# Two more pairs as block products in the last projection, with the weight sums made ahead and kept in HBM

## The chip, the cores and the metric

The kernel runs on one core of a Trainium2 chip. The metric is the device time of one execution in microseconds; the median of three runs before the change is 849.74 us (849.52 to 850.18).

## The reference

One trunk layer on x of 512 tokens by 1024 features, in float32:

```python
xn = rmsnorm(x, norm_mix_g)
q, k, v, xr, gr, ga, gb = split(xn @ w_in)
ya = chunked_band_attention(q, k, v, rel_table) @ w_attn_out
hr = rg_lru(causal_depthwise_conv(xr, conv_w, conv_b), ...)
yb = (hr * gelu(gr)) @ w_rnn_out
h = x + (sigmoid(ga + b_a) * ya + sigmoid(gb + b_b) * yb) @ w_o
hn = rmsnorm(h, norm_ffn_g)
g, up = split(hn @ w_ffn_in)              # 2 x 2816 columns
h = h + (silu(g) * up) @ w_ffn_out        # 2816 -> 1024: the last projection
return rmsnorm(h, final_norm_g)
```

The attention has 16 heads of 64; a frame sees its own chunk of 64 frames and the eight before it.

## The kernel before, in words

Every product of float32 matrices is made of three matmuls on rounded parts. An operand is split into a high part (a ScalarE copy) and a low part (what VectorE's subtraction leaves); mm3 at L76 to L78 multiplies high by high, high by low and low by high into one PSUM bank. A weight therefore goes through three steps: a load into a tile with the tag raw (three buffers, L167), the high part on ScalarE and the low part on VectorE (split, L82 and L83), into a tile with the tag whl.

The stages follow each other: the projections of the recurrent branch and its gates (the loop over j = 0, 2, 4, 6, two feature tiles at a time), q and k of the first head pairs, the recurrent branch's output (yb), v, the attention head by head with one q, k or gate tile between a head's transposes and its weighing, the attention's output, the merge with W_o, and the feed-forward part, whose input projection comes in six units.

Some products of two by two blocks are made with seven block products instead of eight (a scheme of Strassen and Winograd). It needs sums of the weight blocks: with blocks b11, b12, b21, b22 these are t1 = b12 - b11, t2 = b22 - t1, t3 = t2 - b11 and t4 = b21 - t2. For W_o and the first unit of W_ffn_in, sums_kept makes these sums early, inside the loop over j and behind k_tile(0), in four tiles b0 to b3 of the pool ob. It loads the four blocks (L285), subtracts on VectorE (L293 to L296), stores sums to HBM (L299), makes high and low parts of others (L303, L304) and stores them (L306); later stages load them from there. When the pool ob closes, the pool aw of the attention takes its memory; aw holds q and k of every second head pair, and the sums for v.

The last projection multiplies the 2816 activations, 22 tiles of 128 rows in eleven pairs, by W_ffn_out. Five pairs are plain: for each half of the 1024 columns, each of four token tiles and both rows of blocks there are three matmuls of 128x512. Six pairs (paired) are block products, where a block is 128 rows by 512 columns of the weight and 128 features by 256 tokens of the activation. Their weight pieces are fo0 (the first column half), t12 (t1 and t2), t3b (b22 - b12, and b22) and t4; out_sums loads rows of W_ffn_out and subtracts (L223, L225, L231, L237) before the parts are made. a_first, a_sums, a_second and a_last make the parts and sums of the activations. The order on TensorE: the first column half of the plain pairs, fo0 of the paired ones, the second half of two plain pairs, t12, one plain pair, t3b, t4, and two plain pairs last, so that the final norm can follow tile by tile.

What sets the order: in the attention and the feed-forward part TensorE's order, and in the last projection TensorE's and VectorE's, are those of the program text. Everywhere else a planner lists each engine's instructions by its own estimate of when they can start, the earlier in the text first. keep_in_program_order ties an instruction behind the one traced before it on its engine. SP issues nearly all transfers, in one list, and an engine stands still at an instruction whose inputs are late. prefetch makes the weight pieces in the order of the plan, as many pieces ahead as weights(name, ahead) says.

The instruction that follows the stores of the sums of W_ffn_in is the evacuation of k_tile(1): kh by ScalarE (L911), kl by VectorE (L912), in tiles of aw. The sums of x for v (x_sums, L945 and L947) are tied behind kl. whl_yb (L82, L83) are the weights of the recurrent output, v_t (L257, L258) sums of the weights of v, whl_v_t their parts.

In a head of the attention, bias_tile loads a bias of 256 KB (L703), GpSimd sets a corner of it (L704), scores adds it and takes the softmax, GpSimd scales the rows (L1057), and TensorE transposes them (L1068).

Of the kernel before, what the change touches and what calls it, by code (L numbers as in the profile page):

```python
# [8 lines left out]
F32 = mybir.dt.float32  # L9
# [5 lines left out]
P = 128  # L15
# [18 lines left out]
N_PLAIN = 5  # L34
PAIR_TILES = 2 * (11 - N_PLAIN)


@with_exitstack
def block_kernel(ctx: ExitStack, tc: tile.TileContext, x, norm_mix_g, w_in, b_merge, rel_table,
# [137 lines left out]
    t2_of, t2_room = {}, []  # L177
# [17 lines left out]

    def out_sums(name, rows):

        kind, i = name.split("_")
        if kind == "t4":
# [5 lines left out]
        def half_row(col):  # L205
            o = out_room[0].tile([P, S], F32, tag="half", bufs=3, name=f"half_{name}")
            sp.dma_start(out=o[:], in_=w_ffn_out[rows + P:rows + 2 * P, col:col + S])
            return o[:]

        if kind == "t12":  # L210
            raw = wp.tile([P, 2, S], F32, tag="raw", bufs=3, name=f"raw_{name}")
            sp.dma_start(out=raw[:], in_=w_ffn_out[rows:rows + P, :].rearrange("p (c n) -> p c n", c=2))
            b22 = half_row(S)

            if len(t2_of) < 2:
                if not t2_of:
                    t2_room.append(spare[0].tile([P, 2, S], F32, tag="act", bufs=13, name="t2_room"))
                t2 = t2_room[0][:, len(t2_of)]
            else:
                t2 = out_room[0].tile([P, S], F32, name=f"t2_{i}")[:]  # L220
            t2_of[i] = t2
# [4 lines left out]
            high_first(hl[:, 0, 1], hl[:, 1, 1], t1)  # L226
            high_first(hl[:, 0, 0], hl[:, 1, 0], t2)
        elif kind == "t3b":
            raw = wp.tile([P, 2, S], F32, tag="raw", bufs=3, name=f"raw_{name}")
            sp.dma_start(out=raw[:], in_=w_ffn_out[rows:rows + 2 * P, S:].rearrange("(k p) n -> p k n", p=P))  # L230
            dve.tensor_sub(raw[:, 0], raw[:, 1], raw[:, 0])  # L231
            low_parts()
            high_first(hl[:, 0], hl[:, 1], raw[:])
        else:
            b21 = half_row(0)
# [1404 lines left out]
```

## Time and profile before

| | before |
|---|---|
| median of three runs | 849.74 us |
| the profiled execution | 849.69 us |
| its span, first to last instruction | 847.9 us |
| TensorE busy | 839.1 us (99%) |
| VectorE busy | 663.2 us (78%) |
| ScalarE busy | 522.5 us (62%) |
| GpSimd busy | 140.6 us (17%) |
| moved by DMA | 137.17 MB, mean 162 GB/s |

The profile is that of one execution. A line of a timeline has the start in microseconds from the span's start, the duration in microseconds, the engine (PE is TensorE, DVE VectorE, ACT ScalarE, POOL GpSimd, SPq the transfers that SP issues), the line of the kernel, the operation, and what it writes and reads; in brackets stands how long the engine stood idle before it and what ended that. Ends of matmuls are modelled and overlap the next start, so that starts are what to read. The table by stretches gives the busy microseconds and the number of instructions of each engine in a stretch of time.

### The profile page before, as it was taken

The page shows a single profiled execution, that of the slowest core. Times are in us where ns is not written, and L with a number is a line of the kernel's source. Part 1 is how long each engine was busy: PE and PEld are TensorE (multiplying, and loading weights), DVE is VectorE, ACT ScalarE, POOL GpSimd, SP SyncE. Part 2 cuts the span into 40 slices and gives each one's busy share as a digit, 9 for nine tenths or more (in the row PEclk, how much of TensorE's full clock was granted, in tenths as well). Part 3 has the DMA queues.
Part 4 walks back from the last instruction along what each step waited for, and adds up shares of the span by engine and source line. Part 5 has one row for each costly group of instructions (what it writes and reads, how often), then busy time and mean ns, then how long its engine had stood idle before and what let it go on. Part 6 is the DMA issues. An engine that isn't in the chain of part 4 may idle for free.

```text
span 847.9 us, 11598 instructions
## 1 busy us (share of the span) xinstructions
PE 839.1 (99%) x4114; PEld 710.8 (84%) x4114; DVE 663.2 (78%) x972; ACT 522.5 (62%) x864; POOL 140.6 (17%) x179
## 2 busy tenths in 40 slices
PE   9999999999999999999999999999999999999996
PEld 6988888888888888888888888888888999888885
DVE  6667769886999788787568777888778878798995
ACT  7595848774466688787534568654664576645434
POOL 2412030221050133333000000003002213200000
PEclk9999999999999999999999999999999999999999
DMA  8433386777545433222233974555544445526642
GB/s 284 167 104 118 128 298 234 221 266 247 186 137 150 112 100 101 87 75 75 64 110 125 342 295 132 187 163 159 161 152 148 132 138 178 162 75 210 211 137 99
DMA packets 95385, 137.17 MB, mean 162 GB/s; under 512 B 7288, under 2 KB 62160, under 8 KB 94816
## 3 DMA queue, kind: packets, MB, share of 16 engines
q1 hardware_dynamic: 93696, 132.93, 48.9%
q10 hardware_dynamic: 1232, 2.95, 0.9%
q8 instruction: 32, 0.52, 0.3%
q0 software_dynamic: 400, 0.57, 0.3%
q14 instruction: 25, 0.20, 0.1%
HBM read 122.75 MB, written 13.67 MB: 161 GB/s over the span
## 4 chain that ended last, share of the span: by engine, by line
PE 82%; DVE 8%; ACT 4%; DMA 3%; issue 2%; ACTq 0%; DVEq 0%
PE fu_x L78 2%; PE fu_x L76 2%; PE fu_x L77 2%; PE po_out L76 2%; PE po_out L77 2%; PE po_out L78 2%; PE o L1088 2%; PE fg_x L78 2%; PE fg_x L76 2%; PE fg_x L77 2%; PE pT L1068 2%; PE po_ga L78 2%; PE po_ya L78 2%; PE po_ya L77 2%; PE po_ya L76 2%
## 5 line engine op out<-in xcount | busy, mean ns | idle before, releaser
L1288 POOL TENSOR_TENSOR sg<-sg,keep_fu_x 128x512 f32<-128x512 f32 (+1 forms) x10 | 17.8, 1782 | 238.8 <-DVE keep_fu_x L1287 238.8
L1057 POOL TENSOR_SCALAR p<-p,rl 128x128 f32<-128x128 f32 (+3 forms) x61 | 44.0, 739 | 14.9 <-DVE rl L1053 14.0
L1051 DVE CUSTOM_DVE_ANT_0 p<-s,bias 128x128 f32<-128x128 f32 (+1 forms) x64 | 28.6, 485 | 11.6 <-PE s L1043 10.2
L1052 ACT ACTIVATE p<-p,m 128x128 f32<-128x128 f32 (+1 forms) x64 | 35.5, 556 | 2.4 <-DVE m L1051 2.0
L76 PE MATMUL po_out<-whl_fo,act_hi 128*128 128x512 f32 (+1 forms) x80 | 30.9, 386 | 0.0
L78 PE MATMUL po_out<-whl_fo,act_lo 128*128 128x512 f32 (+1 forms) x80 | 30.7, 384 | 0.0
L77 PE MATMUL po_out<-whl_fo,act_hi 128*128 128x512 f32 (+1 forms) x80 | 30.7, 384 | 0.0
L83 DVE TENSOR_TENSOR whl_fu_w<-raw_fu_w,whl_fu_w 128x1024 fp32r<-128x1024 f32 (+1 forms) x18 | 22.1, 1227 | 8.5 <-ACT whl_fu_w L82 8.5
L83 DVE TENSOR_TENSOR pp<-pT,pp 128x384 fp32r<-128x384 f32 (+1 forms) x48 | 26.9, 596 | 2.0 <-ACT pp L82 1.8
L77 PE MATMUL po_xr<-xnT,whl_xr 128*128 128x512 f32 (+1 forms) x80 | 27.7, 353 | 0.0
L83 DVE TENSOR_TENSOR whl_fu_t<-t_fu,whl_fu_t 128x1024 fp32r<-128x1024 f32 (+1 forms) x18 | 23.8, 1324 | 4.8 <-ACT whl_fu_t L82 4.6
L77 PE MATMUL po_gr<-xnT,whl_gr 128*128 128x512 f32 (+1 forms) x80 | 27.5, 347 | 0.0
L78 PE MATMUL po_gr<-xnT,whl_gr 128*128 128x512 f32 (+1 forms) x80 | 27.3, 347 | 0.0
L78 PE MATMUL po_xr<-xnT,whl_xr 128*128 128x512 f32 (+1 forms) x80 | 27.2, 346 | 0.0
L76 PE MATMUL po_gr<-xnT,whl_gr 128*128 128x512 f32 (+1 forms) x80 | 27.1, 347 | 0.0
L76 PE MATMUL po_xr<-xnT,whl_xr 128*128 128x512 f32 (+1 forms) x80 | 26.3, 351 | 0.4 <-ACT xnT L615 0.4
L83 DVE TENSOR_TENSOR whl_fo<-raw_fo,whl_fo 128x1024 fp32r<-128x1024 f32 x16 | 20.7, 1304 | 7.7 <-ACT whl_fo L82 7.7
L82 ACT ACTIVATE whl_fu_w<-raw_fu_w 128x1024 fp32r<-128x1024 f32 (+1 forms) x18 | 17.8, 989 | 13.0 <-issue 7.1
L76 PE MATMUL po_k<-xnT,whl_qk 128*128 128x512 f32 x64 | 25.5, 398 | 0.0
L76 PE MATMUL po_q<-xnT,whl_qk 128*128 128x512 f32 x64 | 25.5, 398 | 0.0
L76 PE MATMUL po_ga<-xnT,whl_ga 128*128 128x512 f32 x64 | 25.4, 397 | 0.0
L82 ACT ACTIVATE whl_fu_t<-t_fu 128x1024 fp32r<-128x1024 f32 (+1 forms) x18 | 17.7, 988 | 12.6 <-PE fu_x L78 9.0
(614 smaller groups left out, 2994.9 us busy)
## 6 DMA issues: line engine op xcount, KB each, us to landing
raw_qk<-in_w_in_dram SPq DMA_DIRECT2D x32, 256.0 KB, 3.2
raw_fu_w<-in_w_ffn_in_dram SPq DMA_DIRECT2D x16, 512.0 KB, 4.4
raw_fo<-in_w_ffn_out_dram SPq DMA_DIRECT2D x16, 512.0 KB, 4.1
raw_xr<-in_w_in_dram SPq DMA_DIRECT2D x8, 512.0 KB, 5.7
raw_gr<-in_w_in_dram SPq DMA_DIRECT2D x8, 512.0 KB, 4.4
raw_ga<-in_w_in_dram SPq DMA_DIRECT2D x8, 512.0 KB, 3.8
raw_gb<-in_w_in_dram SPq DMA_DIRECT2D x8, 512.0 KB, 3.6
o_b<-in_w_o_dram SPq DMA_DIRECT2D x8, 512.0 KB, 6.9
```

What stands on the lines that cost most here:

```text
L76: pe.matmul(o, sh, mh, start=start, stop=False, skip_group_check=parts)
L77: pe.matmul(o, sh, ml, start=False, stop=False, skip_group_check=parts)
L78: pe.matmul(o, sl, mh, start=False, stop=stop, skip_group_check=parts)
L82: act.activation(hi, src, AF.Copy)
L83: dve.tensor_sub(lo, src, f(hi))
L1051: dve.tensor_tensor_reduce(prob[qb][:], scs[qb][:, 0:w], bias[:, S - w:S], -1.0, 3e38, ALU.add, ALU.min, nmax[:, qb:qb + 1])
L1052: act.activation(prob[qb][:], prob[qb][:], AF.Exp, bias=nmax[:, qb:qb + 1], scale=-1.0, accum_out=lsum[:, qb:qb + 1])
L1057: eng.tensor_scalar(prob[qb][:], prob[qb][:], rl[:, qb:qb + 1], 1.0, ALU.mult, ALU.mult)
L1068: pe.transpose(pt[:, at * P:(at + 1) * P], prob[qb][:, kb * P:(kb + 1) * P], ident[:])
L1088: pe.matmul(po[:, S - n:S], st, pp[i][:, part, lo:lo + n], start=kb == 0 and part == 0, stop=kb == NT - 1 and part == 1)
L1288: (pool if keep and (unit != f_units[-1] or side) else dve).tensor_mul(o, o, keep[a] if keep else banks[a])
```

## The change

Three pairs stay plain and eight become block products. The sums of their weights are made ahead by two new functions: out_blocks loads the two rows of blocks of the next pair (two loads of 512 KB), out_sums_kept makes four subtractions of 128x512 on VectorE and stores the result to HBM (two stores of 512 KB). They are called twice at the end of j = 0 and once at the end of j = 2, before sums_kept there, in the tiles b0 to b3 of ob; once between q_tile(0) and k_tile(0) in b2 and b3; and four times in the attention, in two of the three raw tiles: the loads after heads 0, 8, 10 and 12, the subtractions and stores after heads 1, 9, 11 and 13. In the last projection, out_sums loads the kept sums and makes only the high and low parts. The plan of the pieces has one plain pair less in the middle of the second column half. The order on TensorE holds back the second product of the last three pairs (two_sided) and takes t3b in two groups; the preparation of the activations is spread anew, and two activation tiles move into the room of the sums.

```diff
 CW = 256
-N_PLAIN = 5
-PAIR_TILES = 2 * (11 - N_PLAIN)
+N_PLAIN = 3
+PAIR_TILES = 2 * (11 - N_PLAIN) - (4 - (N_PLAIN - 1))
-    for i in plain[:-3]:
+    for i in plain[:-2]:
         plan_out(1, i)
     for i in paired:
         plan_block("t12", i)
-    plan_out(1, plain[-3])
+    out_kept = {i: dr.tile([2, P, D], F32, name=f"out_t{i}") for i in paired}
+    out_raw, t4_raw = {}, {}
+
+    to_keep = list(paired)
+
+    def out_blocks(pl=None, tags=("raw", "raw"), bufs=3):
+
+        i = to_keep.pop(0)
+        out_raw[i] = [(pl or wp).tile([P, 2, S], F32R, tag=tag, bufs=bufs, name=f"raw_out{i}_{n}")[:] for n, tag in enumerate(tags)]
+        out_raw[i] = [f(raw) for raw in out_raw[i]]
+        for n, raw in enumerate(out_raw[i]):
+            at = (2 * i + n) * P
+            sp.dma_start(out=raw, in_=w_ffn_out[at:at + P, :].rearrange("p (c n) -> p c n", c=2))
+
+    def out_sums_kept():
+
+        i = next(iter(out_raw))
+        one, two = out_raw.pop(i)
+        tc.keep_in_program_order(dve.tensor_sub(one[:, 1], one[:, 1], one[:, 0]))
+        dve.tensor_sub(two[:, 1], two[:, 1], one[:, 1])
+        dve.tensor_sub(one[:, 0], two[:, 1], one[:, 0])
+        dve.tensor_sub(two[:, 0], two[:, 0], two[:, 1])
+        for n, raw in enumerate((one, two)):
+            sp.dma_start(out=out_kept[i][n], in_=raw.rearrange("p c n -> p (c n)"))
+
...
+        if kind == "t4":
+            if i not in t4_raw:
+                raw = wp.tile([P, 2, S], F32, tag="raw", bufs=3, name=f"raw_{name}")
+                for n, i_ in enumerate(paired[i - paired[0]:][:2]):
+                    sp.dma_start(out=raw[:, n], in_=out_kept[i_][1, :, 0:S])
+                    t4_raw[i_] = raw[:, n]
+            raw = t4_raw[i]
+        else:
+            raw = wp.tile([P, 2, S], F32, tag="raw", bufs=3, name=f"raw_{name}")
         if kind == "t12":
-            raw = wp.tile([P, 2, S], F32, tag="raw", bufs=3, name=f"raw_{name}")
-            sp.dma_start(out=raw[:], in_=w_ffn_out[rows:rows + P, :].rearrange("p (c n) -> p c n", c=2))
...
-            t1 = raw[:, 1]
-            dve.tensor_sub(t1, raw[:, 1], raw[:, 0])
+            sp.dma_start(out=raw[:], in_=out_kept[i][:, :, S:].rearrange("c p n -> p c n"))
+        elif kind == "t3b":
+            sp.dma_start(out=raw[:, 0], in_=out_kept[i][0, :, 0:S])
+            sp.dma_start(out=raw[:, 1], in_=w_ffn_out[rows + P:rows + 2 * P, S:])
+        else:
             low_parts()
-            dve.tensor_sub(t2, b22, t1)
...
+            high_first(hl[:, 0], hl[:, 1], raw)
             return lambda part, k, at=every: hl[:, part, at]
+        low_parts()
+        high_first(hl[:, 0], hl[:, 1], raw[:])
         return lambda part, k, at=every: hl[:, part, k, at]
@@ loop over j, the recurrent branch @@
+        if j in (0, 2):
+            for tags in (("b0", "b1"), ("b2", "b3"))[j > 0:]:
+                out_blocks(obp, tags, 1)
+                out_sums_kept()
         if j:
             sums_kept(obp, "oof"[j // 2 - 1], (0, 1, 0)[j // 2 - 1])
@@ between the q and k tiles of the first head pair @@
     q_tile(0)
+    out_blocks(obp, ("b2", "b3"), 1)
+    out_sums_kept()
     k_tile(0)
     sums_kept(obp, "f", 1)
@@ attention @@
+    def kept_at(n, where):
+        if n in where and out_raw:
+            out_sums_kept()
+        if n + 1 in where and to_keep:
+            out_blocks()
...
                 probs[h + 2] = scores(h + 2)
             weigh(h, pp)
+            kept_at(h, (1, 9, 11, 13))
@@ last projection @@
+    spare_tags = ["t10", "t11", "t20", "t21"][N_PLAIN - 1:]
     ohp = []
 
     def pair_tile(i, name):
+        if spare_tags:
+            return sums_room.tile([P, 2, 2, 256], F32R, tag=spare_tags.pop(), bufs=1, name=f"{name}{i}")
         return ohp[0].tile([P, 2, 2, 256], F32R, tag="act", bufs=PAIR_TILES, name=f"{name}{i}")
-        todo = [what for i in paired for what in (lambda i=i: a_first(i), lambda i=i: a_sums(i))]
+        firsts = [lambda i=i: a_first(i) for i in paired]
+        sums = [lambda i=i: a_sums(i) for i in paired]
         for i in plain:
...
-                spread(todo, 3)
+                for _ in range(2):
+                    spread(firsts, 1)
+                    spread(sums, 1)
+                spread(firsts, 1)
         pq = [bank("s", f"p_out{a}") for a in range(2)]
-        for n, i in enumerate(paired):
-            w = weights(f"fo0_{i}", 4)
+        last_pairs = paired[-3:]
+
+        def two_sided(one, two, then=None):
+
+            held_ = []
+            for n, i in enumerate(paired):
+                one(n, i)
+                if i in last_pairs:
+                    held_.append(lambda n=n, i=i: two(n, i))
+                else:
+                    two(n, i)
+                if then:
+                    then(n)
+            for what in held_:
+                what()
+
+        pw = {}
+
+        def p_one(n, i):
+            pw[i] = weights(f"fo0_{i}", 4 if n < 4 else 2)
             if n == 0:
                 for t in (2, 3):
                     h_add(0, t, po[t][:])
             for a in range(2):
-                out_block(pq[a][:], left[i], 0, a, w, 0, n == 0)
+                out_block(pq[a][:], left[i], 0, a, pw[i], 0, n == 0)
+            if i == paired[-1]:
+                for a in range(2):
+                    h_add(0, a, pq[a][:])
+
+        def p_two(n, i):
             for a in range(2):
-                out_block(po[a][:], left[i], 1, a, w, 1, False)
+                out_block(po[a][:], left[i], 1, a, pw[i], 1, False)
+
+        def p_then(n):
+            spread(firsts, 1)
+            if n in (1, 3):
+                spread(sums, 1)
+
+        two_sided(p_one, p_two, p_then)
         for a in range(2):
-            h_add(0, a, pq[a][:])
             h_sum(0, a, po[a][:], 0)
         po = [bank("mm", f"po_out1_{t}") for t in range(NT)]
-        ws = [weights(f"fo1_{i}", 2) for i in plain[:-3]]
+        ws = [weights(f"fo1_{i}", 2) for i in plain[:-2]]
 
         for ts in ((2, 3), (0, 1)):
...
+            for i, w in zip(plain[:-2], ws):
                 for t in ts:
                     out_pair(po[t][:], t, i, w, i == 0)
...
         todo = [lambda i=i: a_second(i) for i in paired]
         qq = [bank("t", f"q_out{a}") for a in range(2)]
-        for n, i in enumerate(paired):
-            w = weights(f"t12_{i}", 4)
+
+        def t_one(n, i):
+            spread(sums, 1)
+            pw[i] = weights(f"t12_{i}", 4)
             for a in range(2):
-                out_block(pq[a][:], right_[i], 0, a, w, 0, False)
+                out_block(pq[a][:], right_[i], 0, a, pw[i], 1, False)
+            if i == paired[-1]:
+                for a in range(2):
+                    h_add(1, a, pq[a][:])
+
+        def t_two(n, i):
             for a in range(2):
-                out_block(qq[a][:], right_[i], 1, a, w, 1, n == 0)
-            spread(todo, 1)
+                out_block(qq[a][:], right_[i], 1, a, pw[i], 0, n == 0)
+
+        two_sided(t_one, t_two, lambda n: spread(todo, n > 0))
         for a in range(2):
-            h_add(1, a, pq[a][:])
             h_add(1, 2 + a, qq[a][:])
-        w = weights(f"fo1_{plain[-3]}", 5)
-        for t in range(NT):
-            out_pair(po[t][:], t, plain[-3], w)
-
-        h_add(1, 3, po[3][:, CW:S], slice(CW, S))
+        spread(todo, len(todo))
+        weights(f"t3b_{paired[-1]}", 0)
+        if plain[:-2]:
+            h_add(1, 3, po[3][:, CW:S], slice(CW, S))
         for i in paired:
             a_last(i)
-        weights(f"t4_{paired[-1]}", 0)
+        weights(f"t4_{paired[3]}", 0)
         g_fin = acp.tile([P, D], F32, tag="act", bufs=13, name="g_fin")
         pool.dma_start(out=g_fin[:], in_=final_norm_g.partition_broadcast(P))
...
         ws = [weights(f"t3b_{i}", 0) for i in paired]
-        for w, i in zip(ws, paired):
-            for a in range(2):
-                out_block(pq[a][:], left[i], 0, a, w, 0, False)
-        for a in range(2):
-            h_add(1, 2 + a, pq[a][:])
-        for w, i in zip(ws, paired):
-            for a in range(2):
-                out_block(qq[a][:], left[i], 1, a, w, 1, False)
+        pairs_ = list(zip(ws, paired))
+        for some in (pairs_[:-6], pairs_[-6:]):
+            for w, i in some:
+                for a in range(2):
+                    out_block(pq[a][:], left[i], 0, a, w, 0, False)
+            if some is not pairs_ and len(some) == 6:
+                for a in range(2):
+                    h_add(1, 2 + a, pq[a][:])
+                weights(f"t4_{paired[-1]}", 0)
+            for w, i in some:
+                for a in range(2):
+                    out_block(qq[a][:], left[i], 1, a, w, 1, False)
```

More of the change, by code (lines that the diff above doesn't have):

```diff
@@ L203, in out_sums @@
             hl = out_home(name)
[L205 to L208, printed above, removed]
-        if kind == "t12":
-            raw = wp.tile([P, 2, S], F32, tag="raw", bufs=3, name=f"raw_{name}")
-            sp.dma_start(out=raw[:], in_=w_ffn_out[rows:rows + P, :].rearrange("p (c n) -> p c n", c=2))
[L213 to L221, printed above, removed]
-            t1 = raw[:, 1]
-            dve.tensor_sub(t1, raw[:, 1], raw[:, 0])
-            low_parts()
-            dve.tensor_sub(t2, b22, t1)
[L226 to L235, printed above, removed]
-            t2 = t2_of[i]
-            dve.tensor_sub(t2, b21, t2)
-            low_parts()
-            high_first(hl[:, 0], hl[:, 1], t2)
```

6 lines of the change are left out of this document (3 added, 3 removed).

## The prediction

> **What bounds the kernel now.** I read the first lines of the page, then TensorE's timeline in the last projection, then the busy time by stretches, then who waited for whom around 200 to 250 us, and last the price of each kind of transfer and subtraction.
>
> ```profile
> span 847.9 us, 11598 instructions
> ...
> PE 839.1 (99%) x4114; PEld 710.8 (84%) x4114; DVE 663.2 (78%) x972; ACT 522.5 (62%) x864; POOL 140.6 (17%) x179
> ```
>
> The execution with this span took 849.69 us, so 1.79 us lie around it; the median of the runs is 849.74, 0.05 above. A busy TensorE alone says little, since the modelled ends overlap. The starts of its matmuls say more:
>
> ```profile
> 744.72 0.39 PE L77 MATMUL po_out<-whl_fo,act_hi 128*128 128x512 f32 x1
> ...
> 756.74 0.39 PE L76 MATMUL p_out<-whl_fo,left 128*128 128x512 f32 x1
> ...
> 789.15 0.39 PE L78 MATMUL q_out<-whl_t,right 128*128 128x512 f32 x1
> ```
>
> These are 197 matmuls in a row, all 128x512: 44.43 us over 196 steps, 0.2267 us a step, with no gap. The plain pairs end and the block products begin at 756.74. TensorE sets the time here, and nearly everywhere:
>
> ```profile
> 40.00:60.00 20.00, 20.00 (x94) 16.03 (x93) 12.15 (x15) 17.54 (x25) 2.92 (x3) 1.00 0.43 134
> ...
> 120.00:140.00 20.00, 20.00 (x94) 16.03 (x93) 14.46 (x17) 15.51 (x22) 1.91 (x2) 1.00 0.60 209
> 140.00:160.00 20.00, 20.00 (x90) 16.58 (x89) 18.52 (x21) 11.87 (x16) 6.83 (x5) 1.00 0.90 292
> ...
> 240.00:260.00 20.00, 19.90 (x88) 16.17 (x87) 17.77 (x19) 14.76 (x24) 5.18 (x5) 1.00 0.36 102
> ...
> 740.00:760.00 20.00, 20.00 (x90) 16.57 (x89) 19.58 (x38) 9.47 (x14) 0.00 (x0) 1.00 0.29 98
> ```
>
> After the times come TensorE, its weight loads, VectorE, ScalarE and GpSimd, then clock, DMA share and GB/s. The clock is full, TensorE has its 20 us everywhere, and only 240 to 260 shows a first loss. VectorE is almost full at 140 to 160 and at 740 to 760. So work taken from TensorE is a gain, and work put before a full VectorE or in a chain without slack can eat it.
>
> **The change part by part.** *TensorE's work.* A plain pair is 2 column halves x 4 token tiles x 2 rows of blocks x 3 = 48 matmuls; as block products it is 7 x 2 x 3 = 42. Two more pairs take 12 away: 12 x 0.2267 = 2.72 us. Nothing is added to TensorE. In the section "Back-to-back issue gap" of "TensorE: Matmul & The Clock Gate" the Trainium skill gives about 131 ns for a 512-column matmul in a stream; by it the 12 would be worth 1.57 us. The trace disagrees, with 227 ns.
>
> *Weight sums.* Their unit is a 128x512 subtraction on VectorE; the low part of a weight tile is a 128x1024 one:
>
> ```profile
> 736.87 1.23 DVE L83 TENSOR_TENSOR whl_fo<-raw_fo,whl_fo 128x1024 fp32r<-128x1024 f32 x1 [4.56 <-ACT whl_fo L82]
> 738.01 1.22 DVE L1377 TENSOR_TENSOR act_lo<-act,act_hi 128x1024 fp32r<-128x1024 f32 x1
> ...
> 739.75 0.42 DVE L1442 TENSOR_TENSOR s<-act 128x256 f32<-128x256 f32 x1
> ...
> 741.94 0.69 DVE L83 TENSOR_TENSOR left<-act,left 128x512 fp32r<-128x512 f32 x1
> 742.54 1.22 DVE L83 TENSOR_TENSOR whl_fo<-raw_fo,whl_fo 128x1024 fp32r<-128x1024 f32 x1
> ...
> 769.98 1.23 DVE L83 TENSOR_TENSOR whl_fo<-raw_fo,whl_fo 128x1024 fp32r<-128x1024 f32 x1 [0.84 <-ACT whl_fo L82]
> ```
>
> Start to start, a low part costs 1.14 us (736.87 to 738.01), a 128x512 subtraction 0.60 (741.94 to 742.54), the sums of one activation pair 2.19 (739.75 to 741.94). The projection loses 6 pairs x 4 subtractions x 0.60 = 14.4 us of VectorE. Two pairs more add to it, each, 1.5 low parts of weights (1.7), sums 2.2, two 128x512 parts (1.2) and a 128x256 one (0.35), 5.5 in all, and take away a 128x1024 act_lo (1.14): +8.7. Net 5.7 us less; its transfers stay at 17 MB (6 pairs x 2 + 5 x 1 before, 8 x 1.75 + 3 x 1 after).
>
> *When the pairs begin.* They start two plain pairs, 48 x 0.2267 = 10.9 us, earlier: at 745.86. I counted VectorE's written order from 736.87 on. Up to the low part of the seventh of the eight first-half weights there are six low parts (6.8), eight left parts (4.8), five sums (11.0) and two adds of a bank (1.2): 23.8, so 760.7. TensorE wants it after 66 matmuls, at 760.82; the eighth at 762.2, ready at 761.8. That is a margin of 0.1 to 0.4 us. The row at 769.98 shows VectorE waiting 0.84 us for ScalarE on just such a tile. Bounds: nothing, since the order may leave no wait, and 1.6 (twice that wait); I take 0.5, once 0.84 less 0.4. Later VectorE is ahead: the second half's blocks cost it 1.14 + 0.60 per 12 matmuls (2.72 us), where subtractions came on top before.
>
> *The loop.* Four pairs there: 4 x 2.4 us of VectorE, eight loads and eight stores of 512 KB on SP's queue, all through the four tiles that the sums of W_o and W_ffn_in use. The first round's two pairs fall into 40 to 60, where VectorE has 7.9 us free and the DMA engines are at 0.43; without that cover their 4.8 us would push the low parts of the next weights back. The pair of the second round keeps b2 and b3 until its stores land, so W_o's sums follow about a store and a load later; VectorE has 5.5 us free at 120 to 140 for that. If it doesn't fit, the sums slide into 140 to 160, where the recurrent gates have little room:
>
> ```profile
> 159.09 1.29 POOL L730 TENSOR_TENSOR xch<-xc,xch 128x512 fp32r<-128x512 f32 x1 [4.17 <-issue]
> 161.58 1.66 PE L759 MATMUL rg<-xch,wrg 64*128 64x512 f32 x12
> ```
>
> 1.2 us lie between xch's end and its use. Four subtractions of 1.14 in that stretch would cost at most 4.6 - 1.2 = 3.4. I take 0: the free 5.5 us come first.
>
> *The pair behind q_tile(0).* It is laid between the two sums of W_ffn_in in the same b2 and b3, and those tiles' last store is what the next stage waits for:
>
> ```profile
> 179.77 0.42 SPq L306 DMA_DIRECT2D f_hl<-f_b  x1
> ...
> 185.69 0.37 SPq L285 DMA_DIRECT2D f_b<-in_w_ffn_in_dram  x1
> ```
>
> ```profile
> f_b<-in_w_ffn_in_dram SPq DMA_DIRECT2D x8, 512.0 KB, 5.0
> f_t<-f_b SPq DMA_DIRECT2D x6, 512.0 KB, 4.0
> f_hl<-f_b SPq DMA_DIRECT2D x4, 512.0 KB, 5.9
> ```
>
> ```profile
> 201.42 6.45 DMA f_hl<-f_b
> ...
> 207.95 0.60 ACT kh L911
> ```
>
> ```profile
> 248.84 0.39 PE L76 MATMUL v_z<-whl_v_t,v_s1h 128*128 128x512 f32 x1
> 249.33 0.50 PE L77 MATMUL v_z<-whl_v_t,v_s1h 128*128 128x512 f32 x1
> ```
>
> ```profile
> 208.58 0.68 DVE L912 TENSOR_TENSOR kl<-po_k,kh 64x512 fp32r<-64x512 f32 x1 [4.61 <-ACT kh L911]
> ...
> 210.53 0.69 DVE L912 TENSOR_TENSOR kl<-po_k,kh 64x512 fp32r<-64x512 f32 x1 [0.54 <-ACT kh L911]
> 211.25 1.23 DVE L945 TENSOR_TENSOR v_s<-xnT 128x1024 f32<-128x1024 f32 x1
> 212.39 1.63 DVE L83 TENSOR_TENSOR whl_yb<-raw_yb,whl_yb 128x1024 fp32r<-128x1024 f32 x1
> ...
> 218.07 1.22 DVE L257 TENSOR_TENSOR v_t<-raw_v_t,raw_v_t 128x1024 f32<-128x1024 f32 x1
> ...
> 247.86 1.42 DVE L83 TENSOR_TENSOR whl_v_t<-v_t,whl_v_t 128x1024 fp32r<-128x1024 f32 x1 [1.48 <-ACT whl_v_t L82]
> ```
>
> The tile is free at 185.69; the pair loads (190.7), subtracts (193.1), stores (197.1); W_ffn_in's block loads (202.1), three subtractions of 1.14 (205.5), the store of the one before it (207.3), a copy and a low part at 1.14 each (209.6), the last store 6.45: kh at 216.1 instead of 207.95, 8.1 later. Behind kh wait kl on VectorE and, pinned behind kl, the sums of x for v (v_s, 211.25); at the end of that line TensorE already waits 0.26 us (a step of 0.49 instead of 0.23) for the whl_v_t of 247.86. What can absorb the 8.1: 1.48 us of waiting in that last row and the 0.54 at 210.53, with the smaller gaps between them an estimated 2.6, and, if the planner puts them ahead of kl, two weight tiles and two subtractions for v (4 x 1.14) and a 0.60 evacuation: 5.2. So TensorE loses 8.1 - 2.6 - 5.2 = 0.3 us with the new order and 5.5 with the old. The planner lists what is ready in its own estimate, so a late kh makes it draw the others forward; I take 0.3 and keep 5.5 as the far end. "DMA: Bandwidth & Descriptors" of the Trainium skill, section "Anatomy of one DMA", has a fixed 2.0 us plus bytes at 436 GB/s, 3.2 us for 512 KB; by it the added hops would be shorter, kh about 4.4 us less late (14.0 us of rows against 9.6) and the far end near 1.1. The rows show 4.0 to 6.45, and they decide.
>
> *The attention.* Four pairs, 2.4 us of VectorE each in heads of 9.06 us (362.13 to 371.19, first and last row), four times two loads and two stores on SP.
>
> ```profile
> 362.13 1.28 PE L1068 MATMUL pT<-ident,p 128*128 128x128 f32 x10
> ...
> 362.99 0.34 SPq L703 DMA_DIRECT2D bias<-ext_d  x1
> ...
> 366.20 0.15 POOL L704 MEMSET bias<- 64x64 f32 x1 [7.12 <-DMA bias<-ext_d]
> ...
> 366.44 3.11 POOL L1057 TENSOR_SCALAR p<-p,rl 128x128 f32<-128x128 f32 x4
> ...
> 371.19 1.28 PE L1068 MATMUL pT<-ident,p 128*128 128x128 f32 x10
> ```
>
> GpSimd's memset waits for the head's bias, the scaling behind it ends at 369.55, TensorE's transposes read it at 371.19: 1.6 us to spare. A store pair of 4.0 us right ahead of a bias load costs at most 4.0 - 1.6 = 2.4. Bounds 0 and four such, 9.6; I take 0, as the queue has long empty stretches between biases.
>
> Sum: 849.69 - 2.72 + 0.5 + 0.3 = 847.77, and with the 0.05 to the median 847.8 us.
>
> **The rivals.** *A, the forecast*: the gain arrives but for under 1 us; 847.8, own range 846.7 to 848.0. *B, eaten in small bites*: one bias behind a store pair (2.4) beside the 0.5 and 0.3: 850.2; with half of it 849.0. For it: margins of 0.1 to 1.6 us everywhere. Against: most stretches of SP's queue are empty in the attention. *C, the chain through b2 and b3 keeps its order*: 5.5 us at v, and 849.74 - 2.72 + 0.5 + 5.5 = 853.0. For it: the 4.61 us that VectorE already stands before kl, and the sums pinned behind. Against: 5.2 us of other work can go there. It makes the kernel slower from a loss of 4.4 us on. *D, the removed matmuls weren't the bound*: something else paces the stream, and the end stays, 849.7 plus 0.5. The rule in "Perfetto Trace Analysis" of the Trainium skill, section "Identifying the Most-Contended Engine", says so much: judge by the weight loads' share, here 84%. The trace speaks against D with its 196 equal steps.
>
> **How the numbers follow.** A 0.48, B 0.25, C 0.24, D 0.03. A measurement of this kernel tells about 0.2%, 1.7 us, from no change. Faster by more than that is A; within it B and D, 0.28; slower C. Range: below, the whole 2.72 and the 0.26 at 249.33 regained, 849.74 - 2.98 = 846.76, about 0.25 under it for the measurement: 846.5. Above, it goes to 852.8, just short of C's full price, which leaves out about half of C and little of A.
>
> **What would show it.** TensorE: 12 fewer 128x512 matmuls and the same 0.2267 us step; p_out beginning about 10.9 us earlier relative to po_out, with at most one wait, near its seventh or eighth weight. VectorE: 32 subtractions ahead of 420 us and none in the projection. The row of kh: its wait longer, but whl_yb and v_t ahead of kl. GpSimd's memset: no wait that reaches the transposes. I'm wrong if TensorE stands more than 1 us at v or at yb (C), in the attention (B), or at the gates near 161.

## The result, and the profile after

The changed kernel is slower. Its median is 859.4 us (857.4 to 860.6, six runs) against 849.9 us for the kernel before on the same chip; the ratio is 1.0106, with a 95% interval of 1.0089 to 1.0123, so 9.0 us (7.6 to 10.5). The forecast was 847.8 us, with a range up to 852.8.

The profiled execution took 860.46 us. The first lines of its page:

```profile
span 858.6 us, 11669 instructions
...
PE 841.0 (98%) x4102; PEld 709.3 (83%) x4102; DVE 676.1 (79%) x992; ACT 525.7 (61%) x868; POOL 141.8 (17%) x179
```

The twelve matmuls are gone (4114 to 4102), and the span has grown by 10.7 us. With the 2.72 us of work taken away, TensorE therefore lost 13.4 us, to waits and to a slow clock. The table by stretches (length, TensorE, its weight loads, VectorE, ScalarE, GpSimd, then clock, DMA share, GB/s) says where to look:

```profile
200.00:220.00 20.00, 16.50 (x69) 13.41 (x68) 12.23 (x14) 5.91 (x8) 0.00 (x0) 0.91 0.85 290
240.00:260.00 20.00, 19.44 (x86) 15.74 (x85) 19.34 (x26) 12.37 (x21) 7.29 (x5) 1.00 0.28 90
320.00:340.00 20.00, 19.34 (x105) 16.38 (x104) 15.73 (x37) 14.67 (x33) 6.75 (x13) 1.00 0.52 157
760.00:780.00 20.00, 18.44 (x82) 14.93 (x81) 17.46 (x27) 10.55 (x15) 0.00 (x0) 1.00 0.52 157
800.00:820.00 20.00, 18.35 (x81) 14.75 (x79) 13.89 (x16) 9.67 (x14) 0.00 (x0) 1.00 0.63 204
```

Comparing when the same matmul starts in the two traces gives a ledger. By 200 us the changed kernel is 0.7 late. Of these 0.3 arise in the first 8 us, before any load of a pair (the first is at 24.1), and 0.4 at 128 to 131 us, behind the loop's three pairs. Between 207 and 225 it loses 5.2; at v 0.5; in the attention and just behind it 2.6. It enters the last projection 9.0 late, and that loses 4.3 of its own against its gain of 2.72. In sum 0.7 + 5.2 + 0.5 + 2.6 + 4.3 - 2.7 = 10.6, against the span's 10.7.

**At 207 to 225.** TensorE's rows around its wait, and below them VectorE's and ScalarE's:

```profile
211.38 0.76 PE L76 MATMUL po_yb<-rnn,whl_yb 128*128 128x512 f32 x1 [3.50 <-DVE zb L1138]
211.94 0.63 PE L77 MATMUL po_yb<-rnn,whl_yb 128*128 128x512 f32 x1
212.37 0.63 PE L78 MATMUL po_yb<-rnn,whl_yb 128*128 128x512 f32 x1
...
214.50 0.39 PE L77 MATMUL po_yb<-rnn,whl_yb 128*128 128x512 f32 x1
```

```profile
206.90 1.23 DVE L302 TENSOR_TENSOR f_b<-f_b,f_b 128x1024 f32<-128x1024 f32 x1 [5.67 <-DMA f_b<-in_w_ffn_in_dram]
208.16 1.23 DVE L303 TENSOR_TENSOR f_b<-f_b,f_b 128x1024 f32<-128x1024 f32 x1
209.30 1.22 DVE L304 TENSOR_TENSOR f_b<-f_b,f_b 128x1024 f32<-128x1024 f32 x1
210.55 0.69 DVE L1138 SCALAR_TENSOR_TENSOR zb<-zb,po_yb 128x512 f32<-128x512 f32 x1
```

```profile
216.01 0.59 ACT L923 ACTIVATE kh<-po_k 64x512 fp32r<-64x512 f32 x1 [1.54 <-DMA f_hl<-f_b]
```

The same evacuation of a yb bank in the kernel before, and the matmul that needs the bank:

```profile
202.56 0.69 DVE L1118 SCALAR_TENSOR_TENSOR zb<-zb,po_yb 128x512 f32<-128x512 f32 x1
...
206.82 0.39 PE L76 MATMUL po_yb<-rnn,whl_yb 128*128 128x512 f32 x1
```

VectorE stood 5.67 us at the second subtraction for W_ffn_in, whose block had not landed, and behind it in VectorE's list stood the evacuation zb. That came 8.0 us later than before (202.56 to 210.55). Before, the bank was free at 203.25 and its matmul started at 206.82: 3.6 us of slack. Of the 8.0 us some 4.4 are left over, and the matmul starts 4.6 later than before (211.38); 0.7 of that the kernel was late already. After the wait the matmuls ran at 0.43 us a step up to 214.50, which adds 1.5; 0.2 come back where two products of the scores had been drawn ahead. kh, which the prediction watched, comes at 216.01, and TensorE has no wait behind it before v.

The chain of work that ended last has the reason, and the reasons of the two other losses:

```profile
186.61 4.92 DMA raw_out<-in_w_ffn_out_dram
...
195.41 5.02 DMA out_t<-raw_out
...
200.45 6.33 DMA f_b<-in_w_ffn_in_dram
...
206.90 1.24 DVE f_b L302
...
316.85 4.24 DMA out_t<-raw_out
...
321.53 3.41 DMA raw_qk<-in_w_in_dram
...
760.73 2.28 DVE whl_fo L83 x2
...
763.06 4.67 DMA raw_fo<-in_w_ffn_out_dram
...
770.50 2.35 DVE whl_fo L83 x2
```

Each of the three has the same form: a load starts when the tile's last reader is done, and that was a late store or a late subtraction. Further down the chain of W_ffn_in's sums the last stores were quick, 2.7 us by the median where the kernel before has 5.9:

```profile
f_hl<-f_b SPq DMA_DIRECT2D x4, 512.0 KB, 2.7
```

**In the attention** the tile is one of the three raw tiles. The weights of q and k load behind a pair's store, ScalarE stands on the load in its own order, and the softmax's steps stand behind it; elsewhere TensorE waits for a bank of scores that VectorE has not read:

```profile
325.02 1.06 ACT L82 ACTIVATE whl_qk<-raw_qk 128x1024 fp32r<-128x1024 f32 x1 [2.19 <-DMA raw_qk<-in_w_in_dram]
```

```profile
PE po_k L76 <- DVE m L1065: 1.0, 3, 0.5
```

(In this table of waits: total us, how often, the longest.)

**In the projection** there are two long waits, the first in the list at 807.51 and the second at 771.77:

```profile
PE p_out L76 <- ACT right L82: 1.7, 1, 1.7
PE p_out L77 <- DVE whl_fo L83: 1.6, 1, 1.6
```

The rows before the second of them, on ScalarE, VectorE and TensorE:

```profile
765.20 1.06 ACT L82 ACTIVATE whl_fo<-raw_fo 128x1024 fp32r<-128x1024 f32 x1 [3.19 <-DMA raw_fo<-in_w_ffn_out_dram]
767.75 1.06 ACT L82 ACTIVATE whl_fo<-raw_fo 128x1024 fp32r<-128x1024 f32 x1 [1.49 <-DMA raw_fo<-in_w_ffn_out_dram]
...
769.24 0.61 ACT L82 ACTIVATE right<-s 128x512 fp32r<-128x512 f32 x1
```

```profile
769.89 0.69 DVE L83 TENSOR_TENSOR right<-s,right 128x512 fp32r<-128x512 f32 x1 [1.76 <-ACT right L82]
770.50 1.22 DVE L83 TENSOR_TENSOR whl_fo<-raw_fo,whl_fo 128x1024 fp32r<-128x1024 f32 x1
```

```profile
771.77 0.50 PE L77 MATMUL p_out<-whl_fo,left 128*128 128x512 f32 x1 [1.56 <-DVE whl_fo L83]
```

It is a circle. VectorE's low parts at 760.73 stand behind two sums of activations; only they free raw tiles, so the next load starts at 763.06; ScalarE stands on loads, with the high part of an activation sum (right) behind; VectorE stands on that sum, with the next low parts behind.

For the wait at 807.51 the list names right on ScalarE; the evacuation of the bank (h on VectorE, at 806.68) ends at the same time, and in the traces of two later kernels the same wait is put down to it. Both stand behind loads again: h follows a low part of t3b that waited 1.72 us for its high part, and ScalarE had stood 2.52 us on the load of that.

### The profile page after: what moved, and what is told of

Its sections match the earlier page's. It is cut to its first block, busy times and chain, and to the rows that moved or that the text cites. A ratio compares the mean times of both kernels' runs of the same rounds, so it can differ in the third digit from the quotient of the medians.

```text
span 858.6 us, 11669 instructions
## 1 busy us (share of the span) xinstructions
PE 841.0 (98%) x4102; PEld 709.3 (83%) x4102; DVE 676.1 (79%) x992; ACT 525.7 (61%) x868; POOL 141.8 (17%) x179
## 4 chain that ended last, share of the span: by engine, by line
PE 66%; DMA 13%; DVE 12%; ACT 5%; issue 3%; SPq 0%; ACTq 0%; DVEq 0%
PE fu_x L78 2%; PE fu_x L76 2%; PE fu_x L77 2%; PE fg_x L78 2%; PE fg_x L76 2%; PE fg_x L77 2%; PE po_ya L76 2%; PE po_ga L78 2%; PE po_ya L77 2%; PE po_ya L78 2%; PE po_ga L76 2%; PE po_ga L77 2%; PE o L1102 2%; DMA raw_t<-out_t 2%; DMA o_b<-in_w_o_dram 1%
## 5 line engine op out<-in xcount | busy, mean ns | idle before, releaser
L1071 POOL TENSOR_SCALAR p<-p,rl 128x128 f32<-128x128 f32 (+3 forms) x61 | 46.5, 780 | 23.2 <-DVE rl L1067 22.3
L76 PE MATMUL po_yb<-rnn,whl_yb 128*128 128x512 f32 x64 | 25.8, 402 | 3.5 <-DVE zb L1138 3.5
L77 PE MATMUL po_yb<-rnn,whl_yb 128*128 128x512 f32 x64 | 25.4, 397 | 0.0
L78 PE MATMUL po_yb<-rnn,whl_yb 128*128 128x512 f32 x64 | 25.4, 397 | 0.0
L76 PE MATMUL po_gb<-xnT,whl_gb 128*128 128x512 f32 x64 | 25.4, 396 | 0.0
L76 PE MATMUL po_ya<-aT,whl_ya 128*128 128x512 f32 x64 | 25.1, 392 | 0.0
```

Of the source, the lines that this page charges most:

```text
L76: pe.matmul(o, sh, mh, start=start, stop=False, skip_group_check=parts)
L77: pe.matmul(o, sh, ml, start=False, stop=False, skip_group_check=parts)
L78: pe.matmul(o, sl, mh, start=False, stop=stop, skip_group_check=parts)
L1071: eng.tensor_scalar(prob[qb][:], prob[qb][:], rl[:, qb:qb + 1], 1.0, ALU.mult, ALU.mult)
```

## The experiments

The runs below were made on three other chips, each beside the kernel before, whose medians there were 850.9 to 851.2 us. Differences in us are the ratio less one, times 850, with its interval. Single traces there differ by up to 2 us ahead of the attention, between kernels that are the same up to there; I read an experiment by its ratio and by the waits in the part that it changes.

### The two halves by themselves

The front alone: the kernel before, with the new loads, subtractions and stores in their places and its own projection.

```diff
+    early = list(range(3, 11))
+    to_keep = list(early)
...
+    out_blocks(obp, ("b2", "b3"), 1)
+    out_sums_kept()
     k_tile(0)
```

> The kernel before with its own last projection, to which only the eight early pairs are added (loads, subtractions, stores to HBM in the loop, behind q_tile(0) and in the attention); nothing reads them. T1 with T3 (the pair behind q_tile(0) 5.5, start of the loop 0.7, v 0.5, attention some 2.4): 849.9 + 9.1 = 859.0. Rival (losses in the front are partly made up later by slack of the rest, or were the projection's): 853 to 855.

Measured: ratio 1.0078 (1.0063 to 1.0093), 6.6 us slower. TensorE's waits from 190 to 260 us:

```profile
PE po_yb L76 <- DVE zb L1156: 3.0, 1, 3.0
PE v_z L77 <- DVE whl_v_t L83: 2.3, 2, 1.2
```

The wait for the yb bank is there without the new projection. The total lies between the two expectations, 3.1 to 5.1 us for the rival and 9.1 for the theory, and nearer to the rival's. How the front's loss splits is not the same in every kernel: here v costs 2.3 us, and the wait of 3.0 is followed by no slow matmuls.

The projection alone, without the weight sums (it multiplies by rows of W_ffn_out in their place):

```diff
-    out_kept = {i: dr.tile([2, P, D], F32, name=f"out_t{i}") for i in paired}
+    out_kept = {i: w_ffn_out[2 * i * P:2 * (i + 1) * P, :].rearrange("(c p) n -> c p n", p=P) for i in paired}
-    to_keep = list(paired)
+    to_keep = []
```

> The last projection as in the changed kernel, and nothing in front of it: no pair is loaded, subtracted or stored early, and the projection reads the rows of W_ffn_out where the sums would be (this leaves out the weight sums; sizes and transfers of the projection stay). Theory T2 (the projection loses some 4.3 us of its own against its 2.72 gained, because its weight low parts and first products come too late): 849.9 - 2.7 + 4.3 = 851.5. Rival T2b (the tail loses only because of something that the early work leaves late, or its reads of kept tiles are slower): 847.2, faster than before.

Measured: ratio 1.0001 (0.9989 to 1.0012). The 2.72 us of matmuls are won and lost again inside the projection. Its waits from 735 us on:

```profile
PE p_out L77 <- DVE whl_fo L83: 3.0, 1, 3.0
PE p_out L77 <- DVE whl_t3b L187: 0.6, 1, 0.6
```

T2 holds: the projection loses its gain by itself. By the ratio it loses 2.8 us, in its trace 4.4: from its first matmul to its last are 114.71 us, where the kernel before has 113.03 with twelve matmuls more. That trace is of the slowest of its ten executions (853.78 us).

### The pair behind q_tile(0)

Moved into the attention:

```diff
     q_tile(0)
-    out_blocks(obp, ("b2", "b3"), 1)
-    out_sums_kept()
...
-            kept_at(h, (1, 9, 11, 13))
+            kept_at(h, (1, 5, 9, 11, 13))
```

> The pair that lay behind q_tile(0), in b2 and b3, is made in the attention instead (loads at head 4, subtractions at head 5). Theory T1 (the changed kernel lost some 5.5 us there, because W_ffn_in's block could load into the tile only behind the pair's store, VectorE stood 5.67 us on that load with TensorE's evacuation queued behind it): the 5.5 us come back, about 854, less up to 0.6 for one more pair in the attention; no 3.5 us wait of TensorE for a bank near 211 and a clock of 1.00 in 200 to 220. Rival T1b (the planner's new order around kl and the scores costs it, or the added DMA traffic as a whole): no change, 859.4.

Measured: 1.0083 (1.0056 to 1.0109), 7.1 us slower than before, some 2 us better than the changed kernel. The trace shows no wait from 190 us to v and a clock of 1.00 there; at v it is 0.37 behind the kernel before, where the changed kernel is 5.9. So the loss at 207 to 225 is this pair's. But the fifth pair cost the attention far more than the 0.6 allowed (some 2.5 us more than in the changed kernel's trace). TensorE's waits there:

```profile
PE po_k L76 <- DVE m L1063: 1.7, 5, 0.5
PE o L1100 <- ACT kh L925: 1.1, 2, 0.7
```

In place, but in raw tiles:

```diff
-    out_blocks(obp, ("b2", "b3"), 1)
+    out_blocks()
```

> The pair stays behind q_tile(0), with the same loads, subtractions and stores, but in two of the three raw tiles that the weights are loaded into, not in b2 and b3. T1 (the tile hop): f_b loads at once, as in the kernel before, and VectorE does not stand 5.67 us there; 854 if the weights bear two raw tiles less for some 10 us, up to 859 if they don't. Rival T1b (VectorE's four subtractions or the transfers themselves cost it, wherever they lie): the loss at 207 to 225 stays near 5.5 us whichever tile holds the pair.

Measured: 1.0117 (1.0098 to 1.0136). TensorE's wait and the rows behind it:

```profile
PE po_yb L76 <- DVE zb L1138: 3.6, 1, 3.6
```

```profile
208.07 1.06 ACT L311 ACTIVATE f_b<-f_b 128x1024 fp32r<-128x1024 f32 x1 [2.87 <-DMA f_t<-f_b]
```

```profile
209.16 1.22 DVE L312 TENSOR_TENSOR f_b<-f_b,f_b 128x1024 fp32r<-128x1024 f32 x1 [2.70 <-ACT f_b L311]
210.42 0.69 DVE L1138 SCALAR_TENSOR_TENSOR zb<-zb,po_yb 128x512 f32<-128x512 f32 x1
```

The block was there in time (VectorE does not wait at L302), and the wait is the same, as T1b had it: now the chain is late at its next link, the store that frees a tile for ScalarE's copy, which took 7.6 us (200.35 to 207.97). This corrects T1: the hop through b2 and b3 is one way to be late, not the cause by itself. What the two traces share is that links of the chain of W_ffn_in's sums stand ahead of zb on VectorE, with 3.6 us of slack, and that the pair in this place makes zb 8 us late through either set of tiles. That the pair in this place costs the loss is shown; that the order on VectorE is what turns it into a wait is read from the traces. No run puts zb ahead of the chain, and none has the subtractions without their transfers.

### The attention

The four pairs alone, on the kernel before:

```diff
+    early = list(range(7, 11))
...
             weigh(h, pp)
+            kept_at(h, (1, 9, 11, 13))
```

> The kernel before with its own last projection, and only the four pairs of the attention added (two raw tiles each, subtractions after heads 1, 9, 11 and 13); nothing reads their sums. Theory T3 (these pairs cost the attention some 2.4 us by themselves): 2.4 above before. Rival (they lose only because q, k and v come late from the stage before): 0 to 0.5 above before.

Measured: 1.0040 (1.0026 to 1.0055), 3.4 us. ScalarE stands on the weights' load here too, so the loss is the pairs' own:

```profile
319.07 1.06 ACT L82 ACTIVATE whl_qk<-raw_qk 128x1024 fp32r<-128x1024 f32 x1 [1.98 <-DMA raw_qk<-in_w_in_dram]
```

The same pairs through a tile of their own:

```diff
+            if not pair_room:
+                pair_room.append(rnp.tile([P, 2, 2, S], F32R, tag="big", bufs=4, name="pair_room"))
...
-            kept_at(h, (1, 9, 11, 13))
+            kept_at(h, (1, 9, 11, 12))
```

> As the run before, but the four pairs go through one 8 KB tile of their own, which is free after the projection of v, and not through two of the three raw tiles that the weights of q and k are loaded into (the last pair one head earlier, so that the tile is free for the attention's last output). T3a (the raw tiles: the weights of q and k wait for a pair's store, ScalarE stands 2.19 us on such a load with the softmax behind it): most of the 2.4 us goes, 0.5 to 1.0 above before stays. T3b (VectorE: four subtractions between the softmax's steps keep the banks of the scores): 2.4 as with the raw tiles.

Measured: 1.0007 (0.9996 to 1.0018), 0.6 us. TensorE has no wait in the attention, and ScalarE none for raw_qk. VectorE has the same sixteen subtractions. It was the raw tiles.

### The projection

Seven pairs in place of eight:

```diff
-N_PLAIN = 3
+N_PLAIN = 4
```

> The projection alone, as in the second experiment on it, with seven pairs in place of eight (the rows of W_ffn_out stand for the sums, which leaves out the weight sums; nothing early). Gain of TensorE's work 1.36 us. Theory T2 (the first half of the pairs starts before ScalarE and VectorE have made up the activations' sums; one pair less gives 10.9 us and one pair's splits of room): no stall, 1.36 faster than before, 0.9984. Rival (a fixed cost of the new order, its transfers or its two-sided loops): as slow as with eight, 1 to 3 us above that.

Measured: 1.0073 (1.0045 to 1.0101), worse than with eight, against both theories. The rows:

```profile
PE p_out L77 <- DVE whl_fo L83: 6.6, 2, 3.9
```

```profile
766.17 0.63 ACT L82 ACTIVATE left<-act 128x512 fp32r<-128x512 f32 x1 [4.57 <-PE po_out L77]
```

ScalarE's order isn't written out there. With seven pairs the planner has put high parts of the second half's activations (left, which may be overwritten only when TensorE has read the first half's) ahead of high parts of weights that TensorE needs first. This is another fault than that of the eight pairs, so the run says little on T2.

Eight pairs, two sums of activations later:

```diff
             spread(firsts, 1)
-            if n in (1, 3):
-                spread(sums, 1)
```

> The projection alone with eight pairs (weight sums left out), but two of the activations' sums are made in the second half's products and not among the first half's (5.6 us of VectorE later). Theory T2 (VectorE and ScalarE, in their written order, are what the first products wait for): the wait near 767 to 772 (3.1 us in the trace of the projection alone) goes or falls below 1 us, 1 to 2.5 us faster than the eight pairs. Rival (the loads of the weights through three raw tiles set the pace): the wait stays, as slow as the eight pairs.

Measured: 1.0039 (1.0025 to 1.0054), 3.3 us slower than before and slower than the eight pairs as they were, where T2 expected 1 to 2.5 us faster. The wait near 767 is gone, as T2 said, and comes back later:

```profile
PE p_out L76 <- DVE h L1485: 2.4, 1, 2.4
PE p_out L77 <- DVE whl_t L187: 1.0, 1, 1.0
```

A late engine order was not the whole of it; putting work off only moved the stall. That left the loads.

A fourth raw tile, in the room that the half rows of the old projection had:

```diff
+    def out_raw_tile(name):
+        n = out_loads[0] = out_loads[0] + 1
+        pl, bufs = (out_room[0], 1) if out_room[0] and n % 4 < 1 else (wp, 3)
+        return pl.tile([P, 2, S], F32, tag="raw", bufs=bufs, name=f"raw_{name}")
```

> The projection alone with eight pairs (the rows of W_ffn_out stand for the sums, which leaves out the weight sums), and every fourth load of it goes into a fourth raw tile in the room that the old projection's half rows used. Theory T2c (the loads are late since a raw tile comes free only with VectorE's low part, which stands behind the activations' sums; ScalarE then stands on the load with the activations' high parts behind it, and VectorE on those: a circle through three raw tiles): the 3.1 us wait near 766 falls below 1.5, and the kernel is 1 to 2.7 us faster than with three. Rival T2d (VectorE's and ScalarE's work alone, however early the loads): as with three tiles, 851.2 where before is 851.2.

And a fifth (bufs 2, n % 5 < 2):

> The same with two more raw tiles, of five loads two go there. T2c: at most 0.5 us of waits left in the projection, 2 to 2.7 us faster than with three tiles. T2d: as with three.

Measured: 0.9968 (0.9958 to 0.9977) and 0.9967 (0.9956 to 0.9978). That is 2.7 us faster than the kernel before, the full price of the twelve matmuls; neither trace has a wait of TensorE in the projection, which takes 110.31 us in both, 2.72 less than before. VectorE and ScalarE do the same work as with three tiles. So T2c holds and T2d is out: the circle through three raw tiles is the projection's loss, and one more tile breaks it.

### Together

All three mended: the pair moved, the five pairs in their own tile, the fourth raw tile.

```diff
     q_tile(0)
-    out_blocks(obp, ("b2", "b3"), 1)
-    out_sums_kept()
...
-            kept_at(h, (1, 9, 11, 13))
+            kept_at(h, (1, 4, 7, 10, 12))
```

Beside these lines it has pair_room and out_raw_tile as shown above.

> The changed kernel with all three causes met: the pair behind q_tile(0) is made in the attention, all five pairs there go through one 8 KB tile of their own (subtractions after heads 1, 4, 7, 10 and 12), and the projection has the fourth raw tile. By the theories (loop 0.4, attention 0.4 to 0.8 for five pairs, projection -2.72 plus 0 to 2.7): 848.5 to 851.5 where before is 851.2. If one of the three causes is another: 853 or more.

Measured: 848.5 us against 851.1; ratio 0.9976 (0.9966 to 0.9985), 2.0 us faster than the kernel before and the best of the complete kernels. Its table by stretches, to be read against that of the changed kernel:

```profile
200.00:220.00 20.00, 20.00 (x93) 16.66 (x92) 14.09 (x15) 8.54 (x11) 2.52 (x4) 1.00 0.54 177
...
760.00:780.00 20.00, 20.00 (x90) 16.57 (x89) 17.05 (x26) 10.17 (x17) 0.00 (x0) 1.00 0.47 150
800.00:820.00 20.00, 20.00 (x90) 16.57 (x89) 17.22 (x30) 8.03 (x12) 0.66 (x1) 1.00 0.66 208
```

The changed kernel with the fourth raw tile alone (out_raw_tile, and nothing else):

> The changed kernel with only the fourth raw tile of the projection added. If the losses ahead of the projection (about 9 us) and those in it (4.3 us in the changed kernel's trace) are separate: the changed kernel's 1.0106 less 2.7 to 4.3 us, 856 to 857.5 where before is 851.2, with no wait of TensorE after 735 us. If a late front also shapes the projection: less than 2 us better.

Measured: 1.0055 (1.0035 to 1.0075), 4.7 us, with no wait of TensorE after 735 us. That is 4.3 less than the changed kernel's 9.0.

The changed kernel with the front alone mended (the lines of the mended kernel without out_raw_tile):

> The changed kernel with the pair behind q_tile(0) moved and all five pairs of the attention in their own tile, but the projection as changed, with three raw tiles. By the theories the front loses 0.4 to 1.2 and the projection nothing net or up to 1.5: 851.5 to 853.5 where before is 851.2; 848.5 would say that the projection's raw tiles aren't its cause.

Measured: 1.0027 (1.0011 to 1.0043), 2.3 us; from here to the fully mended kernel are again 4.3 us. The projection's loss is therefore separate from the front's. In the trace its waits are:

```profile
PE p_out L77 <- DVE whl_fo L83: 1.4, 1, 1.4
PE p_out L76 <- DVE h L1493: 1.1, 1, 1.1
```

By the ratios the raw tile is worth 2.8 us where the projection stands alone and 4.3 in both complete kernels; the intervals (about 1 to 1.7 us each way) nearly cover the difference. In the traces the projection with four or five raw tiles takes 110.31 us every time, in four kernels. With three and the same order it takes 113.2 to 115.4 in five, so the tile is worth 2.9 to 5.1 us there. What sets the size of the stall from one execution to the next stays open.

Nine pairs in the mended kernel:

```diff
-N_PLAIN = 3
+N_PLAIN = 2
...
-            kept_at(h, (1, 4, 7, 10, 12))
+            kept_at(h, (1, 3, 5, 7, 9, 11))
```

> The mended kernel with nine pairs as block products in place of eight (six pairs made in the attention, after heads 1, 3, 5, 7, 9 and 11): six matmuls fewer. If nothing else binds: 1.36 us under the mended kernel with eight, 847.2 where that had 848.5. If VectorE's splits now come too late, as only two plain pairs are left ahead of the blocks: 848.5 to 852.

Measured: 1.0054 (1.0036 to 1.0071), slower by 4.6 us than before. TensorE waits for the low parts of t12, and VectorE is full in that stretch:

```profile
PE p_out L77 <- DVE whl_t L194: 5.2, 4, 2.5
```

```profile
780.00:800.00 20.00, 16.18 (x61) 11.89 (x60) 19.59 (x31) 11.30 (x17) 0.00 (x0) 0.91 0.59 190
```

The trace points to VectorE's work itself, busy 19.59 of 20 us while TensorE waits. Nine pairs with another order, or with a fifth raw tile, were not tried.

## Why the prediction was wrong

- *TensorE's work, -2.72*: right. 4102 matmuls, and the projection alone with the fourth raw tile is 0.9968 of before, 2.7 us. Rival D is out.
- *When the pairs begin, +0.5 (bounds 0 and 1.6)*: mis-sized, 4.3 in the changed kernel's trace; alone 4.4 in its trace and 2.8 by the ratio. The place was right (the low part near the seventh pair, 771.77). The count took VectorE as if its inputs were there. It left out that a low part also frees the raw tile for the next load, that such a load takes 3.77 to 5.39 us in this trace, and that ScalarE stands on it with the activations' parts behind. The row that the bound was made of (a low part waiting for ScalarE, 769.98) was a sign of just that circle, still harmless: ScalarE had stood 0.49 us on the load there. "Later VectorE is ahead" failed too, with the wait at 807.51, and for the same reason.
- *The loop, 0*: close; 0.4, at 128 to 131 us. What costs it there was not followed up.
- *The pair behind q_tile(0), +0.3, far end 5.5*: the failed step, and the largest: 5.2. It asked only who waits for the end of the chain, kh. The links themselves stand in VectorE's list, and zb behind them evacuates a bank that TensorE needs 3.6 us after it is freed. I had put "a 0.60 evacuation" among the work that could be drawn ahead of kl; in both traces it stood behind a link that waited. The links were mis-sized as well. The block of W_ffn_in was to land at 202.1, and VectorE took it up at 206.90: the pair's load began 0.9 late, and its subtractions (3.8 against 2.4, with a kl between), its store (5.0 against 4.0) and the block's load (6.3 against 5.0) were each longer. With the forecast's own times zb would have ended near 206.2, an estimate from its sum (205.5) and a 0.69 row, and in time. By that estimate both were needed: the instruction left out, and transfers slower than the rows that they were priced by.
- *What agreed with that step, by luck.* kh came at 216.01, with 216.1 forecast: the chain was 3.6 us late up to its last low part, and the last store took 2.6 us instead of 6.45. Rival C named the same size, 5.5, for v; that the two agree is chance too, since C's was 8.1 less 2.6 of gaps and this is a wait with slow matmuls behind it. The prediction's own sign of being wrong, more than 1 us at yb, did come, but nothing in its working led there. v itself lost 0.5, and that is not shown to be the pair's: ten of the eleven traces of kernels with no pair in this place have that wait of v, at 0.2 to 0.9.
- *The attention, 0 (bounds 0 and 9.6)*: mis-sized, 2.6 in the changed kernel and 3.4 alone. The bounds held it, but by another mechanism: I priced the bias loads behind a store on SP's queue, and what paid was the ring of raw tiles. Two of three were held from a pair's load to the end of its store, across the weights of q and k.
- *How the numbers follow*: B, C and the projection's loss were taken as alternatives. All three came, B by another way than forecast, and they add. A range that lets each happen alone is too short where they do not exclude each other.
- *Two prices beside the rows.* The fit that the prediction quotes from "DMA: Bandwidth & Descriptors" in the Trainium skill, section "Anatomy of one DMA", is made there for transfers that GpSimd issues; these are SP's. And a share of 84% for the weight loads still leaves TensorE the busiest engine, ahead of VectorE's 78%, so the share was no argument for D. Neither entered the sum.

## What to carry to other kernels

When a step is put ahead of a chain, list each instruction that stands behind the step in each engine's order, and price the wait at the first of them that somebody needs, not at the chain's end. A load's start is set by the last reader of its tile: before moving work in front of that reader, count the tiles of the ring, since one more tile was worth 4.3 us here and saved VectorE and ScalarE no work. Work that fits an engine's idle time still needs its own room: four pairs in borrowed tiles cost 3.4 us, in a tile of their own 0.6.

## What the runs showed of the hardware

After some waits TensorE ran at half its pace for a while: 0.43 us a step instead of 0.2267. The granted clock in the traces is 0.50 for such a stretch, in the changed kernel from 211.06 to 214.47, and the stretch lasts 3.41 us in five kernels and twice that, 6.83, in one. It came with each of the four waits of 3.5 to 3.9 us: 6 to 12 matmuls were slow, which adds some 1.5 to 2.8 us to the wait itself. After single waits of 2.7, 3.0 and 3.0 us none was; but 6 or 7 were after one of 2.4 and one of 2.5 us, where a shorter wait had come 4 to 10 us earlier. The slow stretch can begin late, 1.0 us after the wait's end in one kernel and 1.4 in another.

"TensorE: Matmul & The Clock Gate" in the Trainium skill, section "Part 1: The HAM clock gate", has a clock halved after an idle window of some 3.4 us, windows that run freely, and 426.7 ns for a cold matmul of 512 columns. The cold step agrees with the 0.43 here, and the length of the stretches with the window; the waits of 2.4 and 2.5 us are shorter than a window, so that an idle window in full does not explain them. Whether the earlier wait or the place of the wait in a window decides was not tested. A stall near 3 us therefore has a price that jumps: none after three of them, some 1.5 us or more after others.
